# A two-block transformer kernel on one core: six places in a new order

## The chip, the core and the metric

The kernel runs on 1 core of one Trainium2 chip. The metric is the time of one execution in device microseconds. Several runs of the kernel before gave 1577.33, 1580.41 and 1583.56 us, with 1580.41 us as the median.

The core has a matmul engine (TensorE, PE in the profile), a vector engine (VectorE, DVE), a scalar engine (ScalarE, ACT), GpSimd (POOL) and SyncE (SP), which here only starts transfers. Each engine works through its own list of instructions in the order in which the program issued them.

## The reference

Input is one sequence of 256 rows of 1024 numbers in fp32 and a memory of 256 rows. Everything is fp32. What is computed, cut to its core:

```
# first block, DEPTH = 2
for l in range(2):
    x = layer_norm(alpha * x + 0.5 * swiglu(x, gate[l,0], up[l,0], down[l,0]))
    mem_kv = mem @ w_kv_mem[l]
    if l == 0:  u = x @ w_in_conv;  tok = B * causal_conv3(C * x_in)      # short convolution mixer
    else:       u = x @ w_in_mlstm; tok = sigmoid(o) * head_norm(mlstm(q, k, v, gates))
    xa = cross_attention(u[..., -256:], mem_kv)                           # 4 heads of 64
    x = layer_norm(alpha * x + concat(tok, xa) @ w_out[l])
    x = layer_norm(alpha * x + 0.5 * swiglu(x, gate[l,1], up[l,1], down[l,1]))
# second block
h = layer_norm(x)
proj = h @ w_in        # pooling input, conv input, latents of the attention, gates of three branches
y = g0 * pool(...) @ pool_proj + g1 * conv31(...) @ conv_proj + g2 * mla(...) @ mla_proj
h = layer_norm(alpha2 * h + y @ w_out)
e = (p @ ple_proj) * sigmoid(h @ ple_gate)
m = moe(h)             # 16 experts in 4 groups, one group and two experts per row, silu(gate) * up, down
out = layer_norm(alpha2 * h + m + e)
```

The feed-forward (swiglu) has 2816 hidden numbers, 22 units of 128; each expert has 512.

## The kernel before

**Numbers.** A fp32 product is made of three products in a faster format: every operand is split in a high part (a cast on ACT) and a low part (a subtraction on DVE), and the matmul adds high by high, high by low and low by high (`prodB`, lines 605 to 607, and `mm3`, lines 595 to 597).

**Weights.** All weights of the dense layers lie in one array in DRAM, in the order in which they are used, as 404 pieces of mostly 128x1024 numbers (`_pieces`). `_blocks` joins two pieces to a transfer of 1 MB, started by SP into one of three raw buffers. A piece is split by ACT (line 297) and DVE (line 305) into one of 10 slots of a ring. `pump(n)` splits up to n further pieces if the slots are free, so its place in the program sets where in the ACT and DVE lists the two operations stand; the block after the next is requested by the first piece that is cast of a block. The order of `_pieces` has to agree with the order in which the stages ask for their weights.

**Rows and sums.** The 256 rows are two halves of 128. There are four PSUM tiles for products that are evacuated at once (`mm`) and four for sums over many units (`acc`); a new user of a tile waits until its last user has been read.

**First loads** (`setup`, line 560). SP starts ident, the first half of x, block 0 and block 1, the second half of x and block 2, in this order. Block 0 is one piece, because `_blocks` begins a new one at piece 1.

**Feed-forward** (`FFN`, four times). Units 0 and 1 are made as a slab for each half of the rows (`slabA`): TensorE multiplies row blocks by weights that stand side by side, ACT makes silu, DVE multiplies by the up part, and TensorE transposes the result (`slabT`), which is then split. Units 2 to 21 are products with hidden numbers on the partitions (`gu`): 24 matmuls each for gate and up, silu on ACT, product and split on both. `down(f, t)` adds unit f of the hidden numbers to the sums of half t; `both(f)` does it for both halves. Before, the order in `body` is: two or four pumps, the first transpose, unit 2, the second transpose, both(0), both(1), unit 3 and on. In the first feed-forward the pumps ahead are mixed between GpSimd and DVE (`mixed`, "pvpv").

**Conv mixer** (`conv_body`). Sixteen units of 24 matmuls, each followed by its evacuation (`conv_evac`), a pump of two pieces, and one step of the cross attention (`attention`: scores, softmax, transposes with a copy, output), which runs in the background along a written plan (`XA_PLAN`).

**mLSTM mixer** (`ml_body`). Fourteen units with their evacuation inside `ml_unit` (the causal convolution of q and k is three DVE operations per unit), pump, one step of the gates and one of the attention. `ml_out(t)` then forms numerator and denominator for a half, scales it, and normalises each head, on DVE; `ml_out(0)` and `ml_out(1)` stand ahead of the last two value and output products (`ml_vo(2)`), and behind these DVE multiplies by the gate, and TensorE transposes the result (`ml_T`).

**Third mixer** (`m2_body`). The order is planned by strings. `MLA_PLAN` tells per step, between the gate and branch products of `MERGE_PLAN`, which part of the attention runs: s scores with softmax, n normalising, t transposes, o output, each with one of four chains. `TAPS_POOL` and `TAPS_MLA` tell how many of the 31 taps of the wide convolution (three channel groups on DVE in the first string, the fourth group by diagonal matmuls in the second) run at each step. `trig` makes the tables of the rotary positions, `conv_in` forms the convolution's input.

**Experts** (`moe`). `gate_out` and the routing (line 1876 and on) find group, experts and ranks of each row; then rows are gathered by matmuls with a selection matrix (`gather_quad`), and expert after expert runs: up products (line 2026), silu, down products (line 2049), output with weights (`expert_out`, line 2064), and for each pair of experts the sums (`combine`, line 2071). Rows beyond the fixed room of an expert go to a spill part. The experts' weights come in six tiles of 1 MB each and are used as they come, without a split; a tile takes a raw buffer, or a pair of ring slots (named wh and wl), and is freed behind its use (`moe_free`). The last layer norm follows (`last_ln`).

## Time and profile before

| | |
|---|---|
| runs | 1577.33, 1580.41, 1583.56 us |
| profiled execution | 1579.06 us, span 1577.3 us |
| TensorE busy | 1512.0 us (96%), 9703 matmuls |
| VectorE busy | 889.5 us (56%) |
| ScalarE busy | 650.1 us (41%) |
| GpSimd busy | 48.0 us (3%) |
| DMA | 332.96 MB, mean 211 GB/s |
| mean granted TensorE clock | 0.992 |

The page lists, for each group of instructions, the busy time, the mean time of one, and the idle time of its engine just before, with what ended it. "TensorE waits" is such an idle time. The granted clock of a stretch is 1.00 at full speed (2.4 GHz) and 0.50 at the lower level (1.2 GHz). DMA slices give what all transfers moved in a fortieth of the span.

### The profile page before, as it was taken

To read this page: it belongs to the slowest core of one execution; us is meant where nothing else is said; L and a number is where in the kernel's file an instruction comes from. 1 tells how busy PE (TensorE), PEld (TensorE's weight loads), DVE (VectorE), ACT (ScalarE), POOL (GpSimd) and SP (SyncE) were. 2 spreads that over 40 slices of the span, in tenths; PEclk is the share of its full clock that TensorE was granted. 3 is DMA by queue.
4 is the path that set the end of the run, shared out by engine and by line. 5 is a ranking of instruction groups with operands and counts; after the bars stand their busy time and mean duration, and the time that the engine had idled before them with its cause. 6 is when DMAs were issued, how large, how long until landed. Compare 5 with 4: busy or idle time off the path is not lost. (4 is left out here: it accounts for less than half of the span.)

```text
span 1577.3 us, 23657 instructions
## 1 busy us (share of the span) xinstructions
PE 1512.0 (96%) x9703; PEld 1242.7 (79%) x9704; DVE 889.5 (56%) x1412; ACT 650.1 (41%) x1044; POOL 48.0 (3%) x66
## 2 busy tenths in 40 slices
PE   7999999899999999999999999999899999999995
PEld 5999989889999799998878899967799974434432
DVE  5644567674545754558866554568788564222223
ACT  4544435443443443436623443455674431111111
POOL 1000000000000000001001000010000000000001
PEclk9999999999999999999999999999999999999998
DMA  6655445445454545446333545545426676999991
GB/s 258 241 214 187 169 153 214 156 167 209 169 207 161 217 161 213 171 141 231 127 130 153 203 180 206 171 152 184 177 76 243 216 278 249 405 366 416 417 416 40
DMA packets 55984, 332.96 MB, mean 211 GB/s; under 512 B 6320, under 2 KB 6640, under 8 KB 24256
## 3 DMA queue, kind: packets, MB, share of 16 engines
q1 hardware_dynamic: 53424, 319.68, 53.9%
q0 software_dynamic: 1872, 9.52, 1.7%
q10 hardware_dynamic: 576, 2.22, 0.4%
q8 instruction: 77, 1.26, 0.3%
q14 instruction: 35, 0.29, 0.1%
HBM read 330.34 MB, written 1.05 MB: 210 GB/s over the span
## 5 line engine op out<-in xcount | busy, mean ns | idle before, releaser
L305 DVE TENSOR_TENSOR wl<-raw,wh 128x1024 fp32r<-128x1024 f32 (+1 forms) x401 | 476.3, 1226 | 125.4 <-ACT wh L297 125.3
L297 ACT CAST wh<-raw 128x1024 fp32r<-128x1024 f32 (+1 forms) x404 | 403.6, 1044 | 158.3 <-PE acc L597 55.5
L605 PE MATMUL mm<-xh,wh 128*128 128x256 f32 x1608 | 455.4, 283 | 0.0
L606 PE MATMUL mm<-xl,wh 128*128 128x256 f32 x1608 | 452.8, 282 | 0.0
L607 PE MATMUL mm<-xh,wl 128*128 128x256 f32 x1608 | 452.2, 281 | 0.0
L605 PEld LDWEIGHTS mm<-xh,wh 128*128 128x128 f32 x1608 | 304.7, 190 | 5.2 <-issue 2.8
L606 PEld LDWEIGHTS mm<-xl,wh 128*128 128x128 f32 x1608 | 304.4, 189 | 2.2
L607 PEld LDWEIGHTS mm<-xh,wl 128*128 128x128 f32 x1608 | 304.8, 190 | 0.0
L413 ACT ACTIVATE fs<-mm 128x256 f32<-128x256 f32 x80 | 30.8, 385 | 293.3 <-PE mm L607 293.3
L415 DVE TENSOR_TENSOR fm<-fs,mm 128x256 f32<-128x256 f32 x80 | 33.7, 421 | 208.4 <-ACT fs L413 208.4
L595 PE MATMUL acc<-wh,fhh 128*128 128x512 f32 x352 | 140.7, 400 | 3.8 <-ACT fhh L590 3.7
L597 PE MATMUL acc<-wh,fhl 128*128 128x512 f32 x352 | 140.0, 398 | 4.2 <-DVE fhl L591 4.2
L596 PE MATMUL acc<-wl,fhh 128*128 128x512 f32 x352 | 140.2, 398 | 0.0
L597 PEld LDWEIGHTS acc<-wh,fhl 128*128 128x128 f32 x352 | 66.7, 190 | 21.4 <-DVE fhl L591 5.9
L595 PEld LDWEIGHTS acc<-wh,fhh 128*128 128x128 f32 x352 | 67.0, 190 | 19.2 <-ACT fhh L590 6.3
L596 PEld LDWEIGHTS acc<-wl,fhh 128*128 128x128 f32 x352 | 66.9, 190 | 12.7
L591 DVE TENSOR_TENSOR fhl<-fm,fhh 128x256 fp32r<-128x256 f32 x80 | 34.0, 425 | 37.8 <-ACT fhh L590 37.8
L643 POOL TENSOR_TENSOR rs_r<-rs_v,nhalf 128x1 f32<-128x1 f32 (+2 forms) x22 | 17.7, 804 | 1176.5 <-DVE rs_v L641 1129.8
L2030 ACT ACTIVATE es<-mm 128x256 f32<-128x256 f32 x16 | 6.1, 383 | 112.6 <-PE mm L2026 112.6
L590 ACT CAST fhh<-fm 128x256 fp32r<-128x256 f32 x80 | 32.5, 406 | 39.0 <-DVE fm L415 39.0
L624 PE MATMUL mm<-wh,xh 128*128 128x512 f32 x128 | 43.1, 418 | 5.0 <-ACT xh L683 2.5
L2031 DVE TENSOR_TENSOR es<-es,mm 128x256 f32<-128x256 f32 x16 | 6.7, 421 | 71.7 <-ACT es L2030 71.7
(593 smaller groups left out, 2112.7 us busy)
## 6 DMA issues: line engine op xcount, KB each, us to landing
raw<-in_ws_dram SPq DMA_DIRECT2D x197, 1024.0 KB, 4.9
wh<-in_we_dram SPq DMA_DIRECT2D x56, 512.0 KB, 11.2
wl<-in_we_dram SPq DMA_DIRECT2D x56, 512.0 KB, 11.2
w<-in_we_dram SPq DMA_DIRECT2D x22, 1024.0 KB, 11.6
raw<-in_we_dram SPq DMA_DIRECT2D x18, 1024.0 KB, 11.3
gb<-in_lnp_dram POOLq DMA_DIRECT2D x5, 1024.0 KB, 5.1
raw<-in_ws_dram SPq DMA_DIRECT2D x3, 768.0 KB, 4.3
w<-in_wg_dram SPq DMA_DIRECT2D x2, 1024.0 KB, 9.0
```

Of the source, the lines that this page charges most:

```text
L297: self.nc.scalar.copy(h[:, :n], src)
L305: self.eng.tensor_sub(l, src, h)
L415: nc.vector.tensor_tensor(m[:, :n], s[:, :n], ps[:, n:2 * n], op=OP.mult)
L590: self.nc.scalar.copy(h, src)
L591: self.nc.vector.tensor_sub(l, src, h)
L595: mm(out, lh, rh, start=first, stop=False)
L596: mm(out, lh, rl, start=False, stop=False)
L597: mm(out, ll, rh, start=False, stop=last)
L605: mm(out, h[:, c], xh[:, k, s], start=k == 0, stop=False)
L606: mm(out, h[:, c], xl[:, k, s], start=False, stop=False)
L607: mm(out, l[:, c], xh[:, k, s], start=False, stop=k == kn - 1)
L624: mm(ps, self.xh[:, kk, s], h[:, c], start=kk == 0, stop=False)
```

## The change

What it does, place by place:

- `_blocks`: block 1 has one piece as well, and `setup` starts blocks 0, 1 and 2 ahead of the second half of x.
- `FFN`: unit 3 is made ahead of both(0) and both(1), the first transpose stands ahead of the pump, the pump behind the slab (`slabA`) and `mixed` are gone; the piece order follows.
- `conv_body` and `ml_body`: the step of attention (and gates) stands ahead of the evacuation and the pump; `ml_unit` is divided in `ml_unit` and `ml_evac`.
- `ml_out`: one call for both halves, with scaling and normalising on ACT and one rsqrt for all; a generator that stands behind `ml_vo(1)` and is stepped through `ml_vo(2)`.
- third mixer: `trig` behind the first step of `conv_in`, the plan of the attention over more steps, the side taps at other steps.
- `moe`: the part of the routing that sorts the experts (`order`) stands behind the first gather; the output of expert 14 ahead of the spill, the last down product in two parts around a step of the spill, `combine` with the half as the outer loop.

```diff
--- before.py
+++ after.py
@@ -71,10 +71,10 @@
             gu(f)
-            if f == 2:
+            if f == 3:
                 dn(0)
                 dn(1)
-            elif 3 <= f <= NF - last:
+            if 3 <= f <= NF - last:
                 dn(f - 1)
@@ -148,10 +148,10 @@
 MERGE = (0, 2, 1)
-MLA_PLAN = "s0+s1+n0+n1 t0 - o0+t1 - o1+s2+s3+n2+n3 - - - t2 o2+t3 o3"
+MLA_PLAN = "s0 s1+n0 - t0+n1 - o0+t1 - o1+s2 s3+n2 - t2+n3 - o2+t3 o3"
 TAPS_BODY = "1111"
-TAPS_POOL = "1011112302111112", "1011011001110000"
-TAPS_MLA = "1111111010202032", "0111010111000000"
+TAPS_POOL = "1011112302111112", "0000010111010111"
+TAPS_MLA = "1111111010202032", "1111111010000000"
 TAPS_CONV = "2020121032020130", "0000000000000000"
@@ -218,7 +218,7 @@
     for i, p in enumerate(pieces):
-        if n + p[1] > BLOCK or i == 1:
+        if n + p[1] > BLOCK or i in (1, 2):
             blocks.append(cur)
@@ -433,8 +433,6 @@
         self.hA[t] = m
-        if t:
-            self.st.pump(1 if self.li == (0, 0) else 4)
 
@@ -459,19 +457,17 @@
 
-        if self.li == (0, 0):
-            self.mixed("pvpv")
-        else:
-            st.pump(2)
         self.slabT(0)
+        st.pump(2)
         self.gu(2, 0, T)
...
         st.pump(2)
-        both(0)
-        both(1)
         for f in range(3, NF):
...
             st.pump(2)
+            if f == 3:
+                both(0)
+                both(1)
             if f == 8:
@@ -486,12 +482,6 @@
 
-    def mixed(self, engs):
-        for e in engs:
-            self.st.eng = self.nc.gpsimd if e == "p" else self.nc.vector
-            self.st.pump(1)
-        self.st.eng = self.nc.vector
-
     def tail(self, fs=None, engs="v"):
@@ -562,9 +552,8 @@
         nc.sync.dma_start(self.X[0], a["x"][:P])
-        self.st.load(1)
+        self.st.load(2)
         nc.sync.dma_start(self.X[1], a["x"][P:])
-        self.st.load(2)
         self.xh = c.tile([P, KT, T], F32R, name="xh")
@@ -895,9 +884,9 @@
                 self.bg.append(self.attention(self.cp, 0, [self.ct["q", 0], self.ct["q", 1]], *self.xamix, XA_PLAN))
+            self.step()
             self.conv_evac(key, ps)
             self.st.pump(2)
-            self.step()
         self.drain()
@@ -926,11 +915,14 @@
     def ml_unit(self, key):
-        nc, p, ct = self.nc, self.cp, self.ct
-        kind, j = key
         ps = self.mm()
...
         self.st.release(("mi",) + key)
+        return ps
+
+    def ml_evac(self, key, ps):
+        nc = self.nc
+        kind, j = key
         if kind == "xq":
@@ -1039,39 +1031,48 @@
 
-    def ml_out(self, t):
+    def ml_out(self):
         nc, p = self.nc, self.cq
-        nm = []
-        den = p.tile([P, 4], F32, name="den", bufs=2)
-        for j in range(2):
-            o = self.acc()
-            for e in range(2):
-                hd = 2 * j + e
-                out = o[:, e * 256:e * 256 + 193]
-                d = self.Dm[hd]
-                if t == 0:
-                    nc.tensor.matmul(out, d[:, 0:P], self.ve[0][:, hd, :193], start=True, stop=True)
-                else:
-                    nc.tensor.matmul(out, d[:, P:T], self.ve[0][:, hd, :193], start=True, stop=False)
-                    nc.tensor.matmul(out, d[:, T:], self.ve[1][:, hd, :193], start=False, stop=True)
-            nm.append(o)
-            nc.vector.tensor_copy(den[:, 2 * j:2 * j + 2], o.rearrange("p (e n) -> p e n", e=2)[:, :, 192])
-        nc.vector.scalar_tensor_tensor(den, den, -1.0, den, op0=OP.mult, op1=OP.max)
-        nc.vector.tensor_tensor(den, den, self.em[:, t], op=OP.max)
-        nc.vector.reciprocal(den, den)
-        h = self.hout[:, t]
-        st = p.tile([P, 4, 6], F32, name="hst", bufs=2)
-        mv = p.tile([P, 4, 2], F32, name="hmv", bufs=2)
-        for hd in range(4):
-            hs = h[:, hd * 192:(hd + 1) * 192]
-            nc.vector.tensor_scalar_mul(hs, nm[hd // 2][:, (hd % 2) * 256:(hd % 2) * 256 + 192], den[:, hd:hd + 1])
-            nc.vector.bn_stats(st[:, hd], hs)
-        for hd in range(4):
-            nc.vector.bn_aggr(mv[:, hd], st[:, hd])
-        r = self.rsqrt(p, mv[:, :, 1], EPS, 4)
-        for hd in range(4):
-            hs = h[:, hd * 192:(hd + 1) * 192]
-            nc.vector.tensor_scalar(hs, hs, mv[:, hd, 0:1], r[:, hd:hd + 1], op0=OP.subtract, op1=OP.mult)
+        h = [self.hout[:, t].rearrange("p (a n) -> p a n", a=4) for t in range(2)]
+        st = p.tile([P, 2, 4, 6], F32, name="hst")
+        mv = p.tile([P, 2, 4, 2], F32, name="hmv")
+        den = p.tile([P, 2, 4], F32, name="den")
+        for t in range(2):
+            nm, e = [], den[:, t]
+            for j in range(2):
+                o = self.acc()
+                for i in range(2):
+                    hd = 2 * j + i
+                    out = o[:, i * 256:i * 256 + 193]
+                    d = self.Dm[hd]
+                    if t == 0:
+                        nc.tensor.matmul(out, d[:, 0:P], self.ve[0][:, hd, :193], start=True, stop=True)
+                    else:
+                        nc.tensor.matmul(out, d[:, P:T], self.ve[0][:, hd, :193], start=True, stop=False)
+                        nc.tensor.matmul(out, d[:, T:], self.ve[1][:, hd, :193], start=False, stop=True)
+                nm.append(o)
+                nc.vector.tensor_copy(e[:, 2 * j:2 * j + 2], o.rearrange("p (e n) -> p e n", e=2)[:, :, 192])
+            nc.vector.scalar_tensor_tensor(e, e, -1.0, e, op0=OP.mult, op1=OP.max)
+            nc.vector.tensor_tensor(e, e, self.em[:, t], op=OP.max)
+            nc.vector.reciprocal(e, e)
+            for hd in range(4):
+                nc.scalar.activation(h[t][:, hd], nm[hd // 2][:, hd % 2 * 256:hd % 2 * 256 + 192], AF.Identity,
+                                     scale=e[:, hd:hd + 1])
+        for t in range(2):
+            for hd in range(4):
+                nc.vector.bn_stats(st[:, t, hd], h[t][:, hd])
+            for hd in range(4):
+                nc.vector.bn_aggr(mv[:, t, hd], st[:, t, hd])
+        r = self.rsqrt(p, mv[:, :, :, 1].rearrange("p t h -> p (t h)"), EPS, 8).rearrange("p (t h) -> p t h", t=2)
+        nb = mv[:, :, :, 0]
+        nc.vector.scalar_tensor_tensor(nb, nb, -1.0, r, op0=OP.mult, op1=OP.mult)
+        yield
+        yield
+        for t in range(2):
+            for hd in range(4):
+                nc.scalar.activation(h[t][:, hd], h[t][:, hd], AF.Identity, scale=r[:, t, hd:hd + 1],
+                                     bias=nb[:, t, hd:hd + 1])
+        yield
 
@@ -1117,15 +1118,16 @@
         for i, key in enumerate(ML_ORDER[5:19]):
-            self.ml_unit(key)
+            ps = self.ml_unit(key)
             if i == 8:
                 self.load_gb()
+            next(gates, None)
+            if i > 1:
+                next(att, None)
+            self.ml_evac(key, ps)
             if i == 1:
...
             self.st.pump(2)
-            next(gates, None)
-            if i > 1:
-                next(att, None)
         for _ in gates:
@@ -1142,9 +1144,10 @@
         self.hout = self.cq.tile([P, 2, 768], F32, name="big")
-        self.ml_out(0)
-        self.ml_out(1)
+        self.bg.append(self.ml_out())
+        self.step()
         self.ml_vo(2)
+        self.drain()
         for t in range(2):
@@ -1303,9 +1306,9 @@
         self.cos, self.sin = self.rot[:, 0], self.rot[:, 1]
-        self.trig(p0)
         cin = self.conv_in()
         next(cin)
+        self.trig(p0)
         cq = self.cq
@@ -1923,6 +1926,16 @@
         nc.vector.tensor_copy(cb, ps[:, 32:48])
+        self.aff, self.o1, self.cb = aff, o1, cb
+
+    def order(self):
+        nc, misc, p = self.nc, self.misc, self.pe
+        tt, ts, stt = nc.vector.tensor_tensor, nc.vector.tensor_scalar, nc.vector.scalar_tensor_tensor
+        aff, o1, cb, rk = self.aff, self.o1, self.cb, self.rk
+
+        def new(n, *shape):
+            return p.tile([P, 2] + list(shape), F32, name="r_" + n)
+
         wt, sm = new("wt", 16), new("sm", 1)
@@ -2065,8 +2078,8 @@
         ST, _, y = self.pairs.pop(q)
-        for j in range(2):
-            for t in range(2):
+        for t in range(2):
+            for j in range(2):
                 for i in range(2):
@@ -2077,6 +2090,7 @@
         xg = self.gather_quad(0)
+        self.order()
         self.macc = [[self.acc() for _ in range(2)] for _ in range(2)]
@@ -2119,6 +2133,7 @@
             if e == 15:
+                self.expert_out(ps, ps, e - 1)
                 next(spill)
@@ -2128,16 +2143,18 @@
             if e:
-                self.expert_out(ps, ps, e - 1)
+                if e < 15:
+                    self.expert_out(ps, ps, e - 1)
                 self.moe_free([_wtile(e - 1, j) for j in (4, 5)])
...
                     self.bcast(gb[:, i * D:(i + 1) * D], row[i])
+        ps = [self.mm(), self.mm()]
+        self.expert_down(*ps, 15, hT2, range(0, 2))
         next(spill)
-        ps = [self.mm(), self.mm()]
-        self.expert_down(*ps, 15, hT2, range(4))
+        self.expert_down(*ps, 15, hT2, range(2, 4))
         next(spill)
```

## Rows read from the trace of the kernel before

**Rows 1.** The page, section 1 and the DMA rate in slices.
```profile
PE 1512.0 (96%) x9703; PEld 1242.7 (79%) x9704; DVE 889.5 (56%) x1412; ACT 650.1 (41%) x1044; POOL 48.0 (3%) x66
...
GB/s 258 241 214 187 169 153 214 156 167 209 169 207 161 217 161 213 171 141 231 127 130 153 203 180 206 171 152 184 177 76 243 216 278 249 405 366 416 417 416 40
```

**Rows 2.** Waits of TensorE: line, awaited work, us in total, times, longest.
```profile
PE acc L1484 <- ACT pr L1495: 4.4, 1, 4.4
...
PE mm L1081 <- DVE big L1150: 3.4, 1, 3.4
...
PE acc L779 <- DVE tmp L773: 2.7, 2, 2.2
...
PE acc L789 <- ACT tmp L782: 2.1, 1, 2.1
PE acc L595 <- DVE cz L1565: 1.7, 1, 1.7
PE acc L1564 <- ACT pT L1520: 1.6, 1, 1.6
PE mm L2026 <- DVE xg L1998: 1.6, 1, 1.6
...
PE acc L1270 <- DVE tap L1265: 1.4, 1, 1.4
PE acc L758 <- DVE Dm L1023: 1.3, 1, 1.3
...
PE mm L2049 <- DVE X L2064: 1.2, 1, 1.2
```

**Rows 3.** Tile X, first 25 us: X[1]'s issue, transfers from issue to landing.
```profile
L566 SPq DMA_DIRECT2D X<-in_x_dram x1: 431/431/431, 2.6 to 2.6; - x1
...
DMA to landing us min/median/max: 3.5/5.9/8.2
```

**Rows 4.** DVE timeline of the first loads: start, us, instruction, idle before.
```profile
14.42 2.36 DVE L305 TENSOR_TENSOR wl<-raw,wh 128x1024 fp32r<-128x1024 f32 x2 [1.39 <-ACT wh L297]
```

**Rows 5.** Table by stretch: length, busy and count by engine, clock, DMA share, GB/s.
```profile
25.10:42.06 16.96, 13.61 (x78) 11.52 (x76) 13.35 (x14) 11.40 (x17) 5.79 (x2) 0.90 0.45 150
342.25:354.61 12.36, 12.05 (x77) 10.50 (x76) 9.54 (x14) 7.72 (x13) 0.00 (x0) 1.00 0.69 257
531.68:547.44 15.76, 13.85 (x77) 11.36 (x76) 10.41 (x14) 7.81 (x13) 0.00 (x0) 0.89 0.65 236
860.96:877.00 16.04, 12.71 (x77) 10.40 (x76) 9.66 (x15) 8.66 (x14) 0.00 (x0) 1.00 0.84 315
...
1141.60:1145.00 3.40, 3.10 (x13) 2.90 (x14) 0.92 (x4) 1.04 (x7) 0.00 (x0) 0.54 0.41 171
```

**Rows 6.** TensorE timeline of the conv mixer: end of unit 12.
```profile
288.20 0.28 PE L607 MATMUL mm<-xh,wl 128*128 128x256 f32 x1
```

**Rows 7.** DVE timeline of the conv mixer: a softmax, and unit 12's evacuation.
```profile
287.96 0.68 DVE L764 TENSOR_REDUCE xa_mx<-acc 128x2 f32<-128x512 f32 x1
...
290.20 0.62 DVE L773 TENSOR_SCALAR tmp<-tmp,xa_sm 128x256 f32<-128x256 f32 x2
...
295.88 0.41 DVE L870 TENSOR_TENSOR ct_b<-ct_o,mm 128x256 f32<-128x256 f32 x1
```

**Rows 8.** DVE timeline behind the mLSTM output's normalising.
```profile
819.29 4.63 DVE L305 TENSOR_TENSOR wl<-raw,wh 128x1024 fp32r<-128x1024 f32 x4
```

**Rows 9.** DVE timeline of the ordering of experts: first and last instruction.
```profile
1310.45 0.18 DVE L1928 TENSOR_TENSOR r_wt<-r_aff,r_o 128x32 f32<-128x32 f32 x1
...
1317.48 0.16 DVE L1964 TENSOR_SCALAR r_rv<-r_rv 128x2 f32<-128x2 f32 x1
```

**Rows 10.** DMA issues from 1500 to 1535 us: count, size, us to landing.
```profile
raw<-in_we_dram SPq DMA_DIRECT2D x3, 1024.0 KB, 16.4
```

**Rows 11.** SyncE timeline: the issue of expert 15's tile.
```profile
1519.39 1.60 SPq L244 DMA_DIRECT2D raw<-in_we_dram  x2
```

**Rows 12.** TensorE timeline of expert 15: that tile's first matmuls.
```profile
1541.28 1.89 PE L2026 MATMUL mm<-raw,xg 128*64 128x512 f32 x8
```

## The prediction

> **What bounds the kernel now.** I read the page first: the line of busy times and the slices of DMA rate [rows 1]. The reader is to see that TensorE is busy for 1512.0 of 1577.3 us and that no other engine is above 57%. So the change, which leaves the matmuls as they are, can win only what TensorE idles (65.3 us) and what a lower clock costs it. The profiled execution lies 1.35 us below the median of the three runs; I make the sum against its own 1579.06 us and add 1.35 at the end.
>
> The second view was the list of TensorE's waits [rows 2]. It is spread thin: no wait is over 4.4 us, and each stands at one place. That is why the sum goes place by place. The third was the table by stretch [rows 5], where the same work stands four times, at different lengths and granted clocks.
>
> **First loads.** The slab before the first feed-forward needs four 512 KB pieces. They now come as 1 + 2 + 1, the last one in a 1 MB block with a later piece, and behind X[1]. After the change they come as 1 + 1 + 2, all ahead of X[1]. The bytes up to the end of the fourth are then those which now reach to the end of X[1]: issued at 2.6, the longer of the two landings 8.2 us, so 10.8 [rows 3]. From there the two casts (1.0 us each, an estimate after the low's 1.18) and behind the second cast its low put the end of the fourth low at about 14.3, with 0.3 for the hand-overs. Now the fourth low starts at 14.42 and ends near 15.6 [rows 4]: two take 2.36 us, 1.18 each. Gain 1.4, from nothing (if smaller blocks carry less per us) to 2.5 (one 1 MB transfer's time at the 416 GB/s of [rows 1]). X[1] is late by the same bytes and lands near 13.3, and its transposes stand behind the slab in TensorE's order, so nothing waits. All loads after this pair up differently; that is a shift of half a block in a stream which runs at 130 to 260 GB/s for most of the span [rows 1], and I count it at nothing.
>
> The trace first: ident (64 KB), X[0], a block of half a megabyte, one of a megabyte and X[1] are all in by 10.8 [rows 3], so transfers of half a megabyte overlap with their neighbours. The Trainium skill's page "DMA: Bandwidth & Descriptors", section "Measured (HBM→SBUF, 128 partitions, SWDGE, issued from GpSimd)", has a rule against this edit: batch transfers to at least 1 MiB for three quarters of the peak. By the fit of its section "Anatomy of one DMA — SWDGE (gpsimd) path" (2.0 us and the bytes at 436 GB/s) a split megabyte costs 2.0 us more, an estimate from that page, and the sum would be 3.4 us poorer. By the same fit the five transfers above would end near 16 us if each waited for the last; the trace has 10.8, so it does not bear the rule out here.
>
> **Feed-forward units (four places).** From the first slab transpose to the end of the second down product the work is the same in all four (a unit of 48 short matmuls, two products of 12 long ones, and the transposes), and the lengths are 16.96, 12.36, 15.76 and 16.04 us [rows 5]. The second is nearly clean at full clock; without its idle time (12.36 less 12.05 busy, and some 0.2 of pipelining) it is 11.9. So the excess is 5.1, 0.5, 3.9 and 4.1, and it holds the waits there and the granted clock of 0.90 and 0.89 in the first and third. The cause is the order: the two down products stand right behind the second slab transpose, whose split (ACT cast, DVE subtract) is queued behind the lows of pumped pieces. In the first it is worst: GpSimd makes two of the lows there, 5.79 us, and DVE beside it is busy for 13.35 us, where the other three stretches have 9.54 to 10.41 [rows 5]. After the change unit 3 stands between (48 matmuls, about half of the 11.9, 5.9), which is more than the excess at any of the four places. What is late next: in the first feed-forward the two GpSimd lows and the early pump are gone, so the ring is less full, and two lows, u2's and u3's or d1's, come on the path at about 1.2 each: 2.4, an estimate from [rows 4]. Gain there 5.1 − 2.4 = 2.7. In the other three the ring is full from the stage before, and the pump removed behind the slab only moves. Gain 0.5 + 3.9 + 4.1 = 8.5, of which I take off 0.7 for the fourth, whose stream is the densest (315 GB/s [rows 5]) and whose pieces land late in either order: 7.8. Together 10.5; bounds 5 (only waits, no clock, and later lows up to 3.6) and 13.6 (all of it).
>
> **Conv mixer.** The step (a part of the cross attention) is put ahead of the evacuation and the pump. Waits that this aims at: 2.7 and 2.1 us in [rows 2], of which 2.2 and 2.1 stand here and 0.5 in the mLSTM loop. But ACT and DVE lag here: unit 12's last product ends near 288.5 [rows 6] and its evacuation to ct_b runs from 295.88 to 296.29 [rows 7], 7.8 us on. They stay as busy as before, so only what is queued directly ahead of the attention step is won: the softmax's last operations and the copy of the turned tile go ahead of one evacuation (0.4) and two pumped lows (1.2 each, [rows 4]), 2.8 us. I take that. Bounds: 0 (the chain moves along) and 7.3 (both waits, 4.3, and 3.0 if the clock no longer falls behind them, an estimate from the last row of [rows 5], where 3.4 us at 0.54 lose 1.6).
>
> **mLSTM.** In the loop the same swap takes out the wait of L758 on Dm, 1.3, and 0.5 on tmp [rows 2]: 1.8, bounds 0 and 3.3. At the output, TensorE waits 3.4 us for the product with the gate [rows 2], because four lows take 4.63 us from 819.29 ahead of it on DVE [rows 8]. The rewrite moves eight scale and eight normalise operations to ACT, which has less to do, computes one rsqrt instead of two, and puts the last normalise in a step between pieces. The lows and the gate products stay on DVE, behind one another as now; what leaves it ahead of them is one half's scaling and normalising, 768 columns each, 0.9 us by the low's 1.18 per 1024 columns. I take 1.5 of these 1.8, since ACT must have ended them; bounds 0 and 3.4. Together 3.3.
>
> **Third mixer.** The trig part moves behind the first step of conv_in: the 1.4 us of L1270 [rows 2] goes, but I put half a us back, at the transposes of the normalised latent, whose rsqrt chain is next on DVE: 0.9 (−0.5, if trig's own DVE work delays that chain, to 1.4). The side taps come sixteen places earlier in one stage and three in the other: 1.7 on cz and 1.6 on the turned pT go [rows 2], since cz is off DVE's queue by then: 3.3 (0 to 3.3). The attention plan spreads s0, s1, n0, n1 over three steps where one held them; the wait of 4.4 on pr is the longest in the list, because scores 1 need accumulators that scores 0's exponentials hold [rows 2], and the clock of 0.54 behind it costs 1.6 of 3.4 us [rows 5]. With one gate product of 24 short matmuls between (half of unit 3, 2.9), 1.5 of the 4.4 is left, and 2 with a pumped cast ahead of the exponentials; t0 then waits for n0, for which I put 2.3. So 6.0 becomes 4.3: 1.7 (0 to 6). Sum 5.9.
>
> **MoE.** Ordering the experts (wt, permutation, ranks) took DVE from 1310.45 to 1317.64, 7.2 us, ahead of the copy of xg [rows 9], and TensorE waited 1.6 for that [rows 2]. It now runs beside the first expert's up products, which take that long again, so 1.6 goes (0 to 1.6). At the end, the output of expert 14 is put ahead of the spill, and the 1.2 us of L2049 on X goes (0 to 1.2). The combine's new loop order I count at nothing. Sum 2.8.
>
> **The sum.** 1.4 + 10.5 + 2.8 + 3.3 + 5.9 + 2.8 = 26.7. 1579.06 − 26.7 = 1552.4; with 1.35, 1553.7. Forecast 1553 us.
>
> **Rivals.** (A) Everything goes, clock included: 2.5 + 13.6 + 7.3 + 6.7 + 10.7 + 2.8 = 43.6, so 1537. For it: the low clocks of [rows 5] stand in stretches with stalls. Against: the lag of 7.8 us on ACT and DVE in the mixer.
> (B) The chains set the pace: in-order ACT and DVE keep their end times, and only places where an operation changes sides or a queue (first loads, MoE order, the output's scaling, side taps) and half of the feed-forward gains hold: 1.4 + 5.3 + 0 + 1.5 + 3.3 + 2.8 = 14.3, so 1566.
> (C) The expert stream sets the end. It runs at 416 GB/s for the last slices [rows 1]. A tile of expert 15, issued at 1519.39 [rows 11], lands 16.4 us on [rows 10], at 1535.8, and is read from 1541.28 [rows 12]. Only these 5.5 us and the 1.2 at the end are then won: 1579.06 − 6.7 + 1.35 = 1574. Against: the transfers start when TensorE frees a tile, so most of an earlier gain moves the stream too.
> (D) Slower: the step put ahead keeps the PSUM slot of its unit. A soft runs from 287.96 to 290.82 [rows 7], 2.9 us; eight of them (four in each mixer), eight turned copies, four Dm and the gates stand ahead of an evacuation then: 23, and 12 for the others as an estimate, 35 us if each comes on the path. Four slots give three units of 2.97 us (a quarter of 11.9), 8.9, against a lag of 7.8 + 2.9 = 10.7. It decides from the point where more than 22 of these 35 are paid, since the other gains are 22.1 (26.7 less 4.6 here). All of it: 1553.7 + 4.6 + 35 = 1593. For it: 10.7 is more than 8.9. Against: the step was ahead of the next unit's evacuation before too, so the same chain had it, one unit later.
>
> **Chances.** Forecast and its own spread (1545 to 1561) 0.56; A 0.11; B 0.18; C 0.10; D 0.05. Half a per cent, about what a measurement of this kernel can tell from no change, is 7.9 us. Below 1572.5 are forecast, A and B: 0.85. C with some of B's edge is within: 0.10; D is above: 0.05. The range leaves out D, the end of C and of A: 1537 to 1573.
>
> **What would show it.** After: the four stretches of [rows 5], now with unit 3 in them, at 17.8 us in the last three and about 20.2 in the first, all at a clock near 1.00; no wait on Dm, pr under 2.5, xg none; the wait on the gate product at 2. Wrong would be: PSUM waits (L605 on an ACT or DVE evacuation) in the two mixer loops, a wait of L2026 on a weight's transfer, or the first slab later than 15.6.

## The result and the profile after

The changed kernel takes 1560.25 us (median; 1557.07 to 1562.92) against 1580.32 us of the kernel before: ratio 0.9872, 95% interval 0.9845 to 0.9899. Timed again with the experiments below it had 1561.85 us, ratio 0.9888 (0.9858 to 0.9919). The forecast was 1553 us, a gain of 27; the gain is 20.

Lines moved with the edits: the wait on pr is at L1487 (was L1484), the one on the turned tile of the attention at L778 (was L789), on the normalised latent at L1351 (was L1348), on X at L1685 (was L1682), on the gated output at L1082 (was L1081).

The first part of the page and TensorE's waits (line, awaited work, us in total, times, longest), in answer to [rows 1, 2]:

```profile
PE 1509.2 (97%) x9703; PEld 1246.2 (80%) x9704; DVE 881.8 (57%) x1398; ACT 655.3 (42%) x1060; POOL 41.1 (3%) x63
```
```profile
PE acc L778 <- ACT tmp L771: 3.6, 1, 3.6
PE acc L1487 <- ACT pr L1498: 3.5, 1, 3.5
PE acc L1685 <- DVE X L656: 3.4, 3, 2.0
PE acc L1351 <- DVE ot L1337: 3.1, 1, 3.1
...
PE mm L1082 <- DVE big L1153: 1.8, 1, 1.8
...
PE acc L1567 <- ACT tap L1563: 1.2, 1, 1.2
...
PE mm L594 <- DVE big L933: 1.1, 1, 1.1
```

Gone: the waits on Dm, cz, xg, conv_in's tap and the feed-forwards' split (the tap of L1567 is that of the side taps). New or longer: ot, 3.1 where it was 0.64 at the longest, and X, 2.0 where 0.80 was the longest. Single waits of over 3 us are now three, tmp, pr and ot; before they were two, pr and big (the first one on x, 4.9, is in both, and longer than the 4.4 that I gave as the longest).

The table by stretch, columns as in [rows 5]. The first four are the feed-forward stretches, now with unit 3 in them; then two places where the clock was low before; then the three places where it is low now:

```profile
24.40:44.79 20.39, 18.45 (x126) 16.41 (x124) 11.78 (x17) 11.35 (x18) 0.00 (x0) 1.00 0.37 128
337.63:354.80 17.17, 17.17 (x124) 16.15 (x123) 11.72 (x17) 11.11 (x18) 0.00 (x0) 1.00 0.81 293
527.70:544.90 17.20, 17.20 (x126) 16.26 (x125) 11.61 (x17) 10.99 (x18) 0.00 (x0) 1.00 0.80 288
848.30:865.87 17.57, 17.57 (x126) 16.24 (x124) 11.03 (x17) 9.26 (x17) 0.00 (x0) 1.00 0.75 287
35.90:39.40 3.50, 3.50 (x27) 3.32 (x27) 1.19 (x2) 0.39 (x1) 0.00 (x0) 1.00 0.77 279
541.00:544.50 3.50, 3.50 (x17) 2.89 (x16) 2.50 (x5) 2.69 (x4) 0.00 (x0) 1.00 0.51 159
291.50:298.30 6.80, 5.84 (x32) 5.51 (x33) 5.17 (x9) 3.80 (x8) 0.00 (x0) 0.50 0.54 195
1080.00:1086.80 6.80, 6.01 (x19) 5.10 (x20) 5.80 (x10) 2.86 (x6) 0.08 (x1) 0.50 0.44 152
1124.40:1131.20 6.80, 6.05 (x27) 5.85 (x28) 4.82 (x14) 4.57 (x20) 0.00 (x0) 0.50 0.30 98
```

Three feed-forward stretches have no idle time left (length equals busy time). The clock is up at 36 and 541 us, and down longer in the mixers: 1080 is a new place, at 1124 it is down for 6.8 us where the kernel before has 3.4, and at 291 once for 6.8 where that has twice 3.4.

To see where the rest went I took the start of the same matmul (counted along the weight products, whose order is alike at the ends of stages) in two traces. The table gives what each stage wins against the kernel before, in us; e6 and e11 are experiments below, "again" is the second profile of the changed kernel.

| stage | forecast | changed | again | e6 | e11 |
|---|---|---|---|---|---|
| first loads | 1.4 | 0.7 | 1.7 | 1.2 | 2.1 |
| feed-forward 1 | 2.7 | 2.4 | 2.0 | 2.3 | 2.3 |
| conv mixer | 2.8 | 1.6 | 2.8 | 1.2 | 1.9 |
| feed-forward 2 | 0.5 | -0.6 | -0.6 | -0.7 | -0.7 |
| feed-forward 3 | 3.9 | 4.3 | 4.3 | 4.3 | 4.3 |
| mLSTM | 3.3 | 4.3 | 4.3 | 3.5 | 3.5 |
| feed-forward 4 | 3.4 | 5.4 | 5.1 | 3.0 | 3.0 |
| third mixer | 5.9 | -3.2 | -3.5 | 1.2 | 3.2 |
| experts and end | 2.8 | 4.3 | 3.4 | 4.4 | 4.5 |
| sum | 26.7 | 19.1 | 19.4 | 20.3 | 24.0 |

All stages but one come near the forecast. The third mixer is 9 us off. Inside it: +1.8 up to the first product behind the tap's wait; -4.8 over the next 40 products, where the wait on ot and the low clock stand; +3.6 up to the pool's output, of which 1.9 is side-tap work that the new string moved behind this point; -2.0 over the attention, the same 1.9 included, so level there; -1.8 at the norm behind w_out.

### The profile page after: what moved, and what is told of

Its sections match the earlier page's. It is cut to its first block, busy times and chain, and to the rows that moved or that the text cites. A ratio compares the mean times of both kernels' runs of the same rounds, so it can differ in the third digit from the quotient of the medians.

```text
span 1558.2 us, 23655 instructions
## 1 busy us (share of the span) xinstructions
PE 1509.2 (97%) x9703; PEld 1246.2 (80%) x9704; DVE 881.8 (57%) x1398; ACT 655.3 (42%) x1060; POOL 41.1 (3%) x63
## 5 line engine op out<-in xcount | busy, mean ns | idle before, releaser
L594 PE MATMUL mm<-xh,wh 128*128 128x256 f32 x1608 | 455.4, 283 | 1.8 <-DVE big L933 1.1
L594 PEld LDWEIGHTS mm<-xh,wh 128*128 128x128 f32 x1608 | 304.2, 189 | 7.6 <-issue 2.2
L632 POOL TENSOR_TENSOR rs_r<-rs_v,nhalf 128x1 f32<-128x1 f32 (+3 forms) x21 | 16.9, 806 | 1187.9 <-DVE rs_v L630 1143.6
L2077 DVE SCALAR_TENSOR_TENSOR X<-mm,ws,X 64x512 fp32r<-64x512 f32 x32 | 24.0, 750 | 37.3 <-ACT X L2074 36.7
## 6 DMA issues: line engine op xcount, KB each, us to landing
raw<-in_we_dram SPq DMA_DIRECT2D x18, 1024.0 KB, 11.4
```

What stands on the lines that cost most here:

```text
L594: mm(out, h[:, c], xh[:, k, s], start=k == 0, stop=False)
```

## Experiments

**e1: trig back in its old place.**
```
-        cin = self.conv_in(); next(cin); self.trig(p0)
+        self.trig(p0); cin = self.conv_in(); next(cin)
```


> The changed kernel with one edit: trig stands ahead of the first step of conv_in again. Theory T (the rotary tables' DVE chain, now behind conv_in, holds up the casts, lows and the rsqrt chain behind it, and the wait on ot that this makes lets the clock fall): the wait on ot of 3.1 us goes back to about 0.6, the 1.4 us on the tap comes back, TensorE's clock stays at full speed from 1080 to 1087, so the lead over the kernel before is about 18 us where the kv products begin, in place of 15.0; time about 1557.3. Rival U (the clock falls there whatever the order, and the wait is due to the casts whose transfer came late): the wait on ot stays above 2 us and the time stays within 1 us of 1560.25.

1564.4 us, ratio 0.9915 (0.9894 to 0.9936): slower, so T fails, and U as well by its letter, which had the wait stay on ot and the time level. The wait on ot does go, but it stands one place earlier:
```profile
PE acc L1273 <- DVE tap L1268: 3.5, 1, 3.5
```
and the clock falls at that one too, from 1073.9 to 1080.7. By the same products the two orders are level here (14.5 and 15.0 us ahead of the kernel before). What makes e1 slower stands elsewhere: 4.4 of the 4.9 us by which its span is longer are lost behind the norm that follows w_out, where TensorE waits 2.3 for X and the clock is then low from 1275.3 to 1285.5. That trig's place brings this is not shown. Something is late that both orders wait for. ACT in the changed kernel names it (start, length, idle before and its end):
```profile
1062.66 0.84 ACT L297 CAST wh<-raw 128x768 fp32r<-128x768 f32 x1 [1.96 <-PE mm L586]
1067.26 0.83 ACT L297 CAST wh<-raw 128x768 fp32r<-128x768 f32 x1 [3.76 <-DMA raw<-in_ws_dram]
```
It is the last of four pieces for the q projections. Before the change it shared a transfer with the third; now it is first in the next one, which SP issues only at 1062.57.

**e2: the norm's row on GpSimd's queue.**
```
-        self.load_gb(nc.sync)
+        self.load_gb(nc.gpsimd)
```


> The changed kernel with one edit: the gain and bias row of the layer norm behind w_out is loaded from GpSimd's queue, not from SP's. Theory V (the regrouped weight blocks let three expert tiles into SP's queue ahead of this load, and these wait for raw buffers): the load is issued before 1255 in place of 1263, the DVE wait of 2.07 us on gb goes, the wait of TensorE for X goes from 2.0 to about 0.2; time lower by 1.8, about 1558.4. Rival W (the load is slow because the expert transfers share the DMA engines): issued early, but still landing behind 1268, gain under 0.5 us.

In the changed kernel DVE's norm behind w_out waits for this row, and SP's queue shows why (DVE, then SP):
```profile
1270.30 0.75 DVE L655 SCALAR_TENSOR_TENSOR X<-X,ln_mv,gb 128x512 f32<-128x512 f32 x1 [2.07 <-DMA gb<-in_lnp_dram]
```
```profile
1238.52 0.38 SPq L284 DMA_DIRECT2D raw<-in_ws_dram  x1
1253.63 9.24 SPq L244 DMA_DIRECT2D raw<-in_we_dram  x3
1263.03 0.33 SPq L572 DMA_DIRECT2D gb<-in_lnp_dram  x1
```
Three expert tiles stand ahead of it and wait for raw buffers. On the other queue the wait is gone:
```profile
PE acc L1685 <- DVE X L656: 1.6, 3, 0.8
```
and the lead does not drop at that place (17.1 before and behind it, where the changed kernel falls from 16.7 to 14.8). V holds, with 0.8 left where I had written 0.2. 1557.58 us, ratio 0.9869 (0.9852 to 0.9885), which by itself can't be told from the changed kernel's 0.9872.

**e3: the old attention plan.**
```
-MLA_PLAN = "s0 s1+n0 - t0+n1 - o0+t1 - o1+s2 s3+n2 - t2+n3 - o2+t3 o3"
+MLA_PLAN = "s0+s1+n0+n1 t0 - o0+t1 - o1+s2+s3+n2+n3 - - - t2 o2+t3 o3"
```


> The changed kernel with one edit: the attention plan of the kernel before (s0, s1, n0, n1 in one step). Theory P (the new plan wins nothing here, since scores 0's maximum waits behind a DVE backlog and TensorE then idles 3.5 us and runs at the lower clock from 1124 to 1131): the old plan is level or better by up to 2 us, 1558 to 1560.5, with one wait of about 4.5 on pr and a short low-clock stretch. Rival Q (the new plan gives the 1.7 us that I had put on it): slower by 1 to 3 us, 1561.5 to 1563.

1565.28 us, ratio 0.9928 (0.9909 to 0.9947), beyond both. P fails: in the new surroundings the old plan is 5.0 us worse over the attention than the new one (7.0 lost there against 2.0).
```profile
PE acc L1487 <- ACT pr L1498: 6.3, 1, 6.3
...
PE acc L1567 <- ACT pr L1498: 3.1, 1, 3.1
```
So the plan does its work. It is TensorE that comes earlier, by the wait on cz that is gone, and DVE and ACT do not.

**e4: first loads as before.**
```
-        if n + p[1] > BLOCK or i in (1, 2):        self.st.load(2); X[1]
+        if n + p[1] > BLOCK or i == 1:             self.st.load(1); X[1]; self.st.load(2)
```


> The changed kernel with the first loads as before (block 1 of two pieces, the second half of x ahead of block 2), so the weight blocks pair up as before. The first slab transpose comes 0.75 us later. Theory V: the order of SP's queue at the end of the dense layers is the old one, so the load of gb is early again and the 1.8 us behind w_out come back; net faster by about 1.0 us, 1559.2. Rival: the pairing does not matter there, net slower by 0.75, 1561.

1558.29 us, ratio 0.9881 (0.9864 to 0.9897): level with the changed kernel's ratios, so the net is inside the noise. Its trace bears V out: the row is issued at 1255.07 and the wait on ot is down to 1.4. What I had not written: it wins 2.5 us less in the last feed-forward, half of it by the unit lengths of the last section, and 0.7 less in the mLSTM.

**c1: the changed kernel, once more.**

> The changed kernel as it is, on the same chip as the next three, so that they have it beside them. By its first timing its ratio to the kernel before is 0.987. Theory S (the clock falls behind a stall at a moment that differs from execution to execution): the waits of TensorE are the same to 0.3 us, but one or more of the low-clock stretches at 291, 1080 and 1124 us begins or ends elsewhere, and moves the span by 1 to 3 us. Rival: low-clock stretches at the same places and lengths, to 0.5 us.

1561.85 us, ratio 0.9888 (0.9858 to 0.9919). S holds for the waits and the clock: the waits of L778, L1487, L1351 and L1082 agree to 0.2 us, that of L1685 is 1.7 at the longest, and the clock is low for other times and at two more places:
```profile
292.50:295.90 3.40, 3.40 (x19) 3.08 (x15) 2.41 (x6) 2.90 (x6) 0.00 (x0) 0.50 0.72 234
1036.60:1040.00 3.40, 3.40 (x9) 2.62 (x9) 2.33 (x2) 1.36 (x2) 0.00 (x0) 0.50 0.93 265
1081.00:1084.40 3.40, 3.40 (x14) 2.75 (x13) 3.40 (x6) 1.74 (x5) 0.00 (x0) 0.50 0.13 19
1125.40:1128.80 3.40, 3.40 (x18) 3.40 (x17) 2.98 (x9) 1.16 (x6) 0.00 (x0) 0.50 0.21 41
1272.10:1275.50 3.40, 3.40 (x12) 2.83 (x12) 0.91 (x4) 1.32 (x2) 0.00 (x0) 0.51 1.02 418
```
Five stretches of 3.4 us against three of 6.8 in the first profile. The spans are 0.2 us apart, so S's 1 to 3 us do not show on the whole. The conv mixer won 2.8 in this profile and 1.6 in the other, with the same waits.

**e5: fewer taps ahead of scores 0** (with the row on GpSimd's queue).
```
-TAPS_BODY = "1111"   TAPS_POOL "1011..."   TAPS_MLA "1111111010202032"
+TAPS_BODY = "1110"   TAPS_POOL "1001..."   TAPS_MLA "1111111110212032"
```


> The changed kernel with the norm's row on GpSimd's queue, and two steps of the wide convolution's taps (three DVE operations of 0.48 us each) taken from the steps just ahead of and behind scores 0 and put into the next merge. Theory B (DVE's backlog holds up the maximum of scores 0, from 1118.9 when the scores are done to 1122.1): the maximum comes 2.4 us earlier, the wait of 3.5 on pr falls to about 1.1, and the clock does not fall at 1124 or falls for half as long; 2.4 to 5 us faster than with the row on GpSimd's queue alone, so a ratio to the kernel before of 0.983 to 0.985. Rival K (the wait is set by the exponentials' table load and TensorE's own order): the wait stays above 2.8 us, ratio about 0.9865.

The scores are done at 1118.8 in the changed kernel. DVE comes to their maximum behind its backlog:
```profile
1117.77 0.86 DVE L1423 SCALAR_TENSOR_TENSOR yp<-mm,par,yp 128x256 fp32r<-128x256 f32 x2
1118.55 1.21 DVE L305 TENSOR_TENSOR wl<-raw,wh 128x1024 fp32r<-128x1024 f32 x1
1119.68 1.27 DVE L1575 SCALAR_TENSOR_TENSOR cz<-cz,par 128x256 f32<-128x256 f32 x3
1120.87 1.22 DVE L305 TENSOR_TENSOR wl<-raw,wh 128x1024 fp32r<-128x1024 f32 x1
1122.10 0.17 DVE L1492 MEMSET acc<- 64x128 f32 x1
```
1560.08 us, ratio 0.9864 (0.9835 to 0.9893), above what B expected. K fails: the wait on pr is 1.5 at the longest and the clock stays up at 1124. B had 1.1 there, and not the 1.3 that now stands at the turn (L1520). The attention did win 2.0 us in the trace (level, where the changed kernel loses 2.0), but 2.6 were paid back between the attention and the norm: the taps that were put off kept the wide convolution's own norm waiting (0.7 on cz), and the clock fell there, from 1209.6 to 1213.0.

**e6: the old pairing from piece 5 on, new first loads kept.**
```
-        if n + p[1] > BLOCK or i in (1, 2):
+        if n + p[1] > BLOCK or i in (1, 2, 5):
```


> The changed kernel with a further cut of the weight blocks at piece 5, so that from there on two pieces share a transfer as in the kernel before, with the new first loads kept. Theory V2 (the other pairing makes a block late at the third mixer's start and the norm's row late at its end): wait on ot about 1.5 in place of 3.1, no low clock at 1080, the row of the norm early and the wait for X at 0.8, a wait of about 1.2 on fm back in the last feed-forward; 1 to 3 us faster than the changed kernel. Rival: the late block comes from the tighter order of the stages, whatever the pairing: ot above 2.8, time level.

1557.88 us, ratio 0.9850 (0.9821 to 0.9879), timed beside the changed kernel's 1561.85. V2 holds in each part that the trace shows: the row is early, the wait on ot is half, no low clock stands at 1080, and 1.1 us on fm is back in the last feed-forward. Waits, then SP's queue, then the stretch that was at 0.50, and last a wait of the changed kernel:
```profile
PE acc L1685 <- DVE X L656: 1.5, 3, 0.8
PE acc L1351 <- DVE ot L1337: 1.5, 2, 1.3
...
PE acc L956 <- ACT gt_T L952: 1.1, 1, 1.1
PE mm L441 <- DVE fm L434: 1.1, 1, 1.1
```
```profile
1256.16 0.33 SPq L572 DMA_DIRECT2D gb<-in_lnp_dram  x1
1259.96 3.73 SPq L244 DMA_DIRECT2D raw<-in_we_dram  x3
```
```profile
1080.00:1086.80 6.80, 5.27 (x27) 3.84 (x26) 5.46 (x14) 5.85 (x15) 1.04 (x1) 1.00 0.44 154
```
```profile
PE acc L956 <- ACT gt_T L952: 0.3, 1, 0.3
```
The third mixer goes from 3.5 lost to 1.2 won. But the other stages pay: e6 wins 1.6 less in the conv mixer, 0.8 less in the mLSTM and 2.1 less in the last feed-forward than the second profile of the changed kernel (of the 2.1, 1.1 are the unit lengths of the last section). The first two are no accident of two profiles. In those with the new order in the mixers and one low stretch of 3.4 us in the conv mixer, this stage wins 2.8 to 3.0 with the new pairing and 1.2 to 1.9 with the old; the mLSTM wins 4.3 in all with the new pairing and 3.4 to 3.7 in all with the old. So the new pairing took out waits that the kernel before and e6 have, on gt_T and fm among them, and made others in the third mixer. The profiled spans differ by 0.9 us, the medians by 4.0, and the intervals of the two ratios overlap; the mechanism is shown by the rows, its size in the time is not.

**e7: the feed-forward part alone on the kernel before.** Piece order, unit 3 ahead of both(0) and both(1), first transpose ahead of the pump, no mixed pump.

> The kernel before with the feed-forward part of the change alone (unit 3 ahead of the first two down products, the first transpose ahead of the pump, no mixed pump, and the piece order to it). Theory F (this part gives its 11 us by itself): faster by 9 to 12 us, ratio 0.9925 to 0.994, with no low clock at 36 and 541 us. Rival G (part of it is given back at the waits of the mixers, which DVE and ACT set): faster by 4 to 7 us, ratio 0.9955 to 0.9975, with longer waits on tmp, Dm and pr than before.

1572.61 us, ratio 0.9944 (0.9928 to 0.9960), between the two and nearer to F. The clock is up at 36 and 541 us; of the waits that G named only the one on tmp is longer (3.7 where it was 2.1). The trace tells both stories: the four stages win 2.2, -0.6, 4.3 and 4.0, together 9.9 (the forecast was 10.5), and 5.2 are given back in the mixers behind them: conv 1.2, mLSTM 2.7 and third mixer 1.3. In the mLSTM the wait of 3.4 on the gated product is as it was, but the clock falls behind it in this profile, from 820.3 to 827.0, and did not before. So that part may be chance rather than the change; the profiled span is 5.0 us shorter and the median 8.5.

**e8: one more product between scores 0 and scores 1** (on e6).
```
-"s0 s1+n0 - t0+n1 - o0+t1 - ..."
+"s0 - n0+s1 t0 n1 o0+t1 - ..."
```


> The kernel with the old pairing from piece 5 on, and an attention plan that puts one more gate or branch product between scores 0 and scores 1 (s0, nothing, n0 and s1, t0, n1, then as in the change). Theory M (the wait on pr of 3.5 us is one for the accumulators that scores 0's exponentials hold, so a further product of 2.9 us covers it): that wait falls under 1 us, no low clock behind it, t0 waits up to 1.5 us for n0; 2 to 4.5 us faster than the kernel with the old pairing, whose ratio to the kernel before was 0.985, so 0.9825 to 0.984. Rival N (in-order DVE and ACT pay the same time at the next wait): the wait moves to t0 or the taps' sums, time level within 1 us, 0.9845 to 0.9855.

1560.25 us, ratio 0.9871 (0.9850 to 0.9892). M fails. N holds for the waits (that on pr falls from 3.7 to 2.3 in all, and 3.1 stands at the turn), but not for the time, which it had level: the attention loses 5.0 us where e6 loses 2.2, and the clock is low from 1130.9 to 1137.8.
```profile
PE acc L1520 <- ACT pr L1508: 3.1, 1, 3.1
...
PE acc L1487 <- ACT pr L1498: 2.3, 2, 2.1
```

**e9: conv step behind evacuation and pump again** (on e6).
```
-            self.step(); self.conv_evac(key, ps); self.st.pump(2)
+            self.conv_evac(key, ps); self.st.pump(2); self.step()
```


> The kernel with the old pairing from piece 5 on, and the conv mixer's step behind evacuation and pump as in the kernel before. Theory C (the new place merges the two waits of 2.2 us into one of 3.6 on the copy, since the in-order chain on ACT and DVE binds): two waits of 2 us or more come back, the conv mixer takes 0.5 to 1.5 us longer without counting the clock; ratio 0.985 to 0.9865. Rival D (the step ahead of the evacuation holds PSUM tiles and costs what it gains): waits of the unit products on ct_x and ct_b (0.9 us) go, mixer level or shorter, ratio under 0.985.

1558.68 us, ratio 0.9862 (0.9840 to 0.9883), against 0.9850 for e6: not told apart by time. In the trace the conv mixer is 1.7 us longer (0.5 lost where e6 wins 1.2), both with one low-clock stretch of 3.4 us there. The waits:
```profile
PE acc L778 <- ACT tmp L771: 4.0, 2, 3.7
...
PE acc L768 <- DVE tmp L762: 2.3, 1, 2.3
```
C holds in kind: the change takes out the 2.3 and leaves the 3.6. The 1.7 is a little over C's 1.5.

**e10: trig back, with the block in time** (on e6).

> The kernel with the old pairing from piece 5 on, and trig ahead of conv_in's first step again. With the block in time, the step as I had it: trig's move takes the wait of 1.4 us on the tap and gives half a us back at ot, so undoing it costs 0.9 us (0.986). Rival: the two waits are one for the same DVE chain (tap 2.5 and more in place of ot 1.3) and undoing costs 0 to -0.5 us in the trace, outside of low-clock stretches (ratio 0.985).

1558.03 us, ratio 0.9857 (0.9835 to 0.9879): no difference in time. The waits are 1.4 on the tap and 0.8 on ot, where e6 has none and 1.5. So trig's move wins 0.7 us here, with 0.9 forecast; the rival's 2.5 on the tap is not there.

**e11: taps moved to places on both sides, none put off to the end** (on e6).
```
-TAPS_BODY = "1111"   TAPS_POOL "1011..."   TAPS_MLA "1111111..."
+TAPS_BODY = "1210"   TAPS_POOL "1001..."   TAPS_MLA "2111111..."
```


> The kernel with the old pairing from piece 5 on, with one step of the wide convolution's taps moved from just behind the pool's projections to the q projections before, and one from the first gate product to the next merge's first step, so that all taps are done where they were. Theory B again (DVE's backlog ahead of the maximum of scores 0): the wait of 3.5 on pr falls to about 1.3, and unlike with the taps put at the end of the next merge, nothing is paid back at the norm of the wide convolution; 2 us faster than the same kernel without it, ratio 0.9825 to 0.984. Rival N (the chains of ACT and DVE bind over the whole attention, so a wait taken at one place stands at the next): the sum of the waits on pr and pT stays within 0.7 us of 3.6, time level, 0.985 to 0.986.

1555.23 us, ratio 0.9838 (0.9824 to 0.9851): the fastest of all. The step of the maximum starts at 1119.22 (its MEMSET, at 1122.10 in the changed kernel), and the long wait is now two short ones:
```profile
PE acc L1487 <- ACT pr L1498: 1.8, 2, 1.5
...
PE acc L1520 <- ACT pr L1508: 1.3, 1, 1.3
```
```profile
1122.00:1129.00 7.00, 5.26 (x37) 4.41 (x37) 5.02 (x15) 4.76 (x20) 0.00 (x0) 1.00 0.20 82
```
Their sum, 3.1, is only 0.6 below e6's 3.7, so for the waits N was nearer than B. The 2.0 us that the attention wins over e6 are mostly the clock, which stays up.

## Why the prediction was right, and where it failed

**Feed-forward units: right.** Forecast 20.2 and 17.8 for the stretches, measured 20.39 and 17.17, 17.20, 17.57. In the first, TensorE waits 2.0 us in all, on lows and a cast, where I had put 2.4 for two lows. The sum of the four stages is 11.4 with 10.5 forecast. Within that, stages 2 and 4 are off by -1.1 and +2.0. The -1.1, and as much of the +2.0, is no stall: see the last section. The rest of the +2.0 is about the wait on fm, which the new pairing took out (0.8 in the kernel before, 1.1 in e6); that is luck, since I had pieces landing late there in either order.

**First loads, the term itself: right in sign, its size open.** I put 1.4, and by the term's own figures it is 1.3. The first product with the fourth piece's low starts 0.7 and 1.7 us earlier in the changed kernel's two profiles; over the eleven profiles with the new order of blocks the mean is 1.2 (0.5 to 2.1). With the old order it is 0.1 in e7 and 0.7 in e4, which undoes the first loads alone, and the eleven differ among themselves by more than the term. The Trainium skill's page "DMA: Bandwidth & Descriptors", section "Measured (HBM→SBUF, 128 partitions, SWDGE, issued from GpSimd)", has the rule to batch transfers to at least 1 MiB, which speaks against the split. No profile here shows such a loss.

**The step that failed: "All loads after this pair up differently ... I count it at nothing".** I looked at the rate of the stream and not at who stands in its queue. The pairing decides which piece of a stage waits for the next transfer, and which transfers SP has ahead of the norm's row. e1 shows that the wait on ot was not trig's, e2 that the row was late by SP's order, e6 that the pairing makes both: restoring it alone turns the third mixer from 3.5 lost to 1.2 won. Of the 9 us missing there this is 4.7. The same pairing had won some 3 us in the conv mixer, the mLSTM and the last feed-forward (e6). In the profiled spans the nothing came out nearly true, at 0.9 us: two errors of opposite sign, which is luck.

**Third mixer, side taps and attention plan: sized for the old surroundings.** I had summed 1.7 for cz, 1.6 for pT and 1.7 for the plan as if independent; of these 5.0 the lead shows 1.6 (from 15.0 to 16.6). The wait on cz did go, but not as I wrote: in the pool's stage the side taps come later, not sixteen places earlier. Before, their first eight products stand just ahead of the one that waits; now they stand behind it (two lines of the kernel before, one of the changed kernel):
```profile
1128.49 1.89 PE L1564 MATMUL acc<-cz,tap 128*128 128x256 f32 x8
...
1132.45 0.39 PE L595 MATMUL acc<-yp,wh 128*128 128x256 f32 x1 [1.71 <-DVE cz L1565]
```
```profile
1136.84 1.97 PE L1567 MATMUL acc<-cz,tap 128*128 128x256 f32 x8 [0.31 <-issue]
```
The 1.6 on pT is gone, and 1.2 stands on the side taps' own tap. Against the old plan the new one wins 5.0 where I put 1.7 (e3): TensorE, without the wait on cz, comes sooner to the scores, and the old plan then waits 6.3 on pr where it waited 4.4. Against the kernel before, the attention wins nothing. The wait on pr was to be under 2.5 and is 3.5, since the maximum of scores 0 stands behind DVE's low parts and taps (rows of e5), which I had not counted. e8 shows that spreading alone moves the wait, e5 and e11 that lightening DVE takes out the part that the clock charges.

**Conv and mLSTM: right in direction.** The chain of ACT and DVE bound the conv mixer as argued: one wait goes, one of 3.6 stays, 1.7 us by e9 where I took 2.8. The 3.6 is not made by the step's new place: e7 and e9, with the old order, have 3.7 there, where the kernel before has 2.1. The stage's 1.6 and 2.8 in the two profiles hold 1 us or more that is the pairing's (e6). The mLSTM loop won 2.7 (1.8 forecast; 1.9 in e6, so the rest is the pairing), the output 1.6 (1.5), its wait 1.8 (2 forecast).

**Experts and end: the forecast was low by 1.5** (by 0.6 in the second profile, where the clock falls at 1272). 1.7 for the order of experts (1.6), 1.9 for the end (1.2), and 0.7 for the combine and last norm that I had counted at nothing.

**Rivals.** A needed the clock to stay up; without the end of the kernel it was down 20 us in total in the changed kernel (three times 6.8) where the kernel before had five stretches of 3.4. B was right for the third mixer's attention and not elsewhere. C is refuted: the lead is 16.5 us from 1346 on and is kept to the end, so the stream moved along. D's mechanism exists, at 1.1 and 0.3 us of waits for PSUM tiles in the two loops (L594, on an evacuation), far from the 22 it needed.

## What to carry to other kernels

An edit at the head of a stream that regroups its transfers is an edit at every later stage, for gain or loss: list which piece now waits for the next transfer, and what stands in the issuing queue ahead of each other load. Gains of neighbouring stages that wait for the same two engines don't add; take the latest of them as the bound, and look for work on these engines that can go to a place before, not after. A long wait can cost more than its length, since the clock can fall with it: waits of 1.8 and 1.3 us with the clock up were 2.0 us cheaper than 3.7 with the clock down (e11 against e6, a profile of each).

## What the runs showed of the hardware that I had not expected

The low clock came with every wait of 3.0 us or more at the four places where one stood in the conv and third mixers (on tmp at L778, tap, ot, pr), always in these profiles. It began between 2.6 us before the wait's end (the 6.3 of e3) and 1.9 us behind it (ot in e2). Its length was 3.4 us in some and 6.8 in others for the same kernel and the same waits. At the gated product of the mLSTM, 3.4 us brought it in one of two profiles. Behind shorter waits it came in some and not in others: at 1036 us, where TensorE waits 2.5 for a low, in the second profile of the changed kernel and not in the first, and in e1 for 10.2 us at 1275, behind waits of 2.3 and 0.8 on X. No run here tells what decides.

A feed-forward unit with both down products takes either 8.43 to 8.44 or 8.50 us (spacing of its silu on ACT), the same for the whole of a stage: stage 2 has 8.43 before and 8.50 after the change, stage 4 8.50 and 8.43, both with TensorE without idle time and at full clock. That makes 1.1 to 1.2 us per stage in either direction: the -1.1 of stage 2 in the table and over half of the +2.0 of stage 4. In stage 2 all thirteen later profiles have 8.50. In stage 4 the edits do not decide it: e1 and e5, which are the changed kernel up to there, have 8.50, and e8, which is e6 up to there, has 8.43 where e6 has 8.50. What sets it is open.
